# Three chunks of 344 tokens in place of four of 258 in the first half of both output projections

## The chip, the cores and the metric

The kernel runs on one core of a Trainium2 chip. The metric is the device time of one execution in microseconds; before the change it is 2502.07 us, the median of three runs (2500.52, 2502.07 and 2508.82).

## The reference

One inference step of a decoder trunk with two layers, 1024 prompt tokens and 8 decode tokens (one for each of 8 sequences), model width 1024. Each sub-layer adds a gated branch to the residual stream, the gate computed from a conditioning vector:

```
h = h + gate(c) * F(rmsnorm(h) * (1 + scale(c)) + shift(c))
```

In the first layer F is an HGRN2 recurrence with 8 heads of 128, in the second a sliding-window attention (window 128, 16 query heads on 4 key-value heads, sinks, relative bias, a cache for the decode tokens). Each ends in an output projection of 1024 by 1024, which is what the change touches:

```
return o.reshape(bsz, t, D_MODEL).astype(xn.dtype) @ w_o, s_new
```

Each mixer is followed by a SwiGLU feed-forward sub-layer of inner width 2816. Outputs are the trunk's outputs for prompt and decode tokens, the recurrent states and the key-value caches.

## The kernel before

Activations lie with the features on the 128 partitions (8 tiles of 128 features, called k or n) and the tokens along the columns. The 1032 tokens, the decode tokens last, are cut in chunks: `G3` has three of 344 columns, `G4` four of 258. Every product of 128 by 128 weights with a chunk is done as three matmuls (`mm3`, lines 291 to 293), with weights and activations each split in a high and a low part.

The output projection is cut in two halves by its inner dimension: `wo_first` multiplies the first four of the eight mixer outputs, `wo_second` the last four. `wo_first` runs while the mixer's last heads are still being computed: the function `run` takes turns between it and other generators in the proportion of the weights beside them. This happens twice. In stage A (lines 1650 to 1653, about 539 to 634 us) it stands beside the last recurrence head (`hgrn_tail`) and a conditioning product. In stage B (line 1988, about 1613.5 to 1727 us) it stands beside the prompt attention (`second`) and the decode attention (`dec`).

For each chunk and each output tile n, `wo_product` does four `mm3`, that is 12 matmuls, into one PSUM bank. The pool of these banks, `mm`, has four. Then `residual` (line 845, on VectorE) multiplies the bank by the gate and adds it to the residual tile in place; that frees the bank. In the last chunk a further update of 8 columns (line 849) takes the decode tokens.

The residual stands in a `Stack` made on `G4`: eight tiles `hs`, one for each chunk of 258 tokens and each group of four features k. `reload_stack` loads them from DRAM on the queue of SyncE (line 658). In stage A all eight loads come before `run`. In stage B it is a generator in two steps: the two tiles of chunk 0 first, then, after the first steps of `second` and `dec` have issued their own loads on the same queue, the six tiles of chunks 1 to 3. The loads between are the attention's (lines 1854 and 1845), the key and value caches (line 1769) and the new decode rows, which overwrite a row of the cache tiles (line 1774). The decode attention's first matmuls are transposes of the cached keys (line 1781), products with the decode queries (line 1789) and scores of the prompt attention beside them (line 1872). `wo_second` and everything after it stay on `G4` tiles of the residual.

Of the kernel before, what the change touches and what calls it, by code (L numbers as in the profile page):

```python
# [12 lines left out]
ALU = mybir.AluOpType  # L13
# [40 lines left out]
G3, G4 = Grid(344), Grid(258)  # L54
# [11 lines left out]
def trunk_kernel(  # L66
# [40 lines left out]
    pe, act, dve, pool, sp = nc.tensor, nc.scalar, nc.vector, nc.gpsimd, nc.sync  # L107
# [10 lines left out]
    def nm(s):  # L118
        uid[0] += 1
        return f"{s}_{uid[0]}"  # L120

    def big(dt=F32, cols=TOK, parts=P):
        return p4.tile([parts, cols], dt, tag="c4", name=nm("c4"))

    def mmp():
        return pp.tile([P, 512], F32, tag="mm", name=nm("mm"), bufs=4)
# [8 lines left out]
    def axp():  # L135
        return pp.tile([P, 512], F32, tag="ax", name=nm("ax"), bufs=4)

    def small(shape, tag, bufs=2, dt=F32):
        return sm.tile(shape, dt, tag=tag, name=nm(tag), bufs=bufs)
# [8 lines left out]
    class Stream:  # L148
# [15 lines left out]
        def next(self):  # L164
            n, room = self.used + 1, self.look
            while n < len(self.specs) and self.size[n] <= room:
                room -= self.size[n]
                n += 1
            self.ahead(n)
            u = self.done[self.used]  # L170
            self.used += 1
            return u
# [238 lines left out]
    for kk in range(4):  # L411
        t = big(cols=1024)
        wa[0].append(first_half(2 * kk, 0, t))
        t = big(cols=1024)
# [12 lines left out]
    ps = axp()  # L427
# [4 lines left out]
    ps = axp()  # L432
# [16 lines left out]
    res = []  # L449
    hd = cst.tile([P, KT, NB], F32, name="hd")  # L450
    xs = dp.tile([KT, P, T], F32, name="xs")
    ps = axp()
# [4 lines left out]
    ada = cst.tile([P, 112, 9], F32, name="ada")  # L457
# [6 lines left out]
    def ada_step(q, k):  # L464
        u = ca.next()
        if k == 0:
            ada_ps[q] = axp()
        for i in range(2):
            for j in range(4):
                pe.matmul(  # L470
                    ada_ps[q][32 * j : 32 * j + 32, 256 * i : 256 * i + 256],
                    cT[:, k, :],
                    u[i][:, j, :],
                    start=(k == 0 and i == 0),
                    stop=(k == KT - 1 and i == 1),
                    tile_position=(0, 32 * j),
                )

    def ada_end(q):
        a = big(cols=512)  # L480
        act.copy(a, ada_ps.pop(q))
        yield
        ps = axp()
        for b in range(4):
            pe.transpose(ps[:, b * P : (b + 1) * P], a[:, b * P : (b + 1) * P], ident)
        psv = ps.rearrange("p (b j r) -> p b j r", b=4, j=4)
        for b in range(4):
            dve.tensor_tensor(
                adav[:, q, :, b, :],
                psv[:, b, :, 0:9],  # L490
                bc(bTv[:, q, :, b], 2, 9),
                op=ALU.add,
            )
# [33 lines left out]
    def mod_scale(m, ks=slice(0, KT)):  # L527
        _, sc, nw = MODS[m]
        return dve.scalar_tensor_tensor(
            modA[:, m, ks, :],  # L530
            ada[:, sc : sc + KT, :][:, ks, :],
            1.0,
            bc(nT[:, nw : nw + KT][:, ks], 2, 9),
            op0=ALU.add,
            op1=ALU.mult,
        )
# [94 lines left out]
    class Stack:  # L631
# [16 lines left out]
        def at(self, k, g, c):  # L648
            return self.t[c][k // self.m][:, k % self.m, : g.pl[c]]

        def move(self, dram, cs, load):
            for c in cs:
                n, s = self.g.pl[c], self.g.prompt(c)
                for i in self.groups():
                    d = dram[self.rows(i)][:, :, s].rearrange("k p n -> p k n")
                    if load:
                        self.t[c][i] = p4.tile([P, self.m, self.g.w], F32, tag="c4", name=nm("hs"))
                        sp.dma_start(self.part(c, i, n), d)
                    else:
                        sp.dma_start(d, self.part(c, i, n))  # L660
# [180 lines left out]
                yield 1  # L841

    def residual(ps, c, n, gate, tdec, g=G3):
        hc = res[-1].at(n, g, c)
        dve.scalar_tensor_tensor(  # L845
            hc, ps[:, : g.pl[c]], ada[:, gate + n, 0:1], hc, op0=ALU.mult, op1=ALU.add
        )
        if c == g.last:
            dve.tensor_tensor(tdec[:, n, :], ps[:, g.pl[c] : g.w], ada[:, gate + n, 1:9], op=ALU.mult)

    def residual_dec(tdec):
        dve.tensor_tensor(hd, hd, tdec, op=ALU.add)
# [431 lines left out]
    def run(*gens):  # L1284


        left = [[0, g, n] for g, n in gens]
        while left:
            x = min(left, key=lambda e: e[0] / e[2])
            r = next(x[1], "end")  # L1290
            if r == "end":
                left.remove(x)
                continue
            x[0] += r or 1
# [44 lines left out]
    def conditioning(quads, mods):  # L1339

        for q in quads:
            for k in range(KT):
                ada_step(q, k)
                if k % 2:
                    yield
            yield from ada_end(q)
            yield
        for m in mods:
            mod_scale(m)


    def mixed(scr, i):

        o = Rows(4)
        for c in range(NCH):
            n = G3.pl[c]
            for k in range(4):
                xh, xl = (z[:, :n] for z in o.at(k, G3, c))
                t = small([P, W], "w", 6)[:, :n]
                sp.dma_start(t, scr[4 * i + k][:, G3.prompt(c)])  # L1360
                act.copy(xh, t)
                eng = dve if k % 2 or not i else pool
                eng.tensor_tensor(xl, t, xh, op=ALU.subtract)
        return o
# [4 lines left out]
    def wo_product(u, o, c, n, gate, tdec, g=G3, bank=mmp):  # L1369
        ps = bank()  # L1370
        for k in range(4):
            i = 2 * k + n % 2
            xh, xl = o.at(k, g, c)
            mm3(ps[:, : g.w], wcol(u, 0, i), wcol(u, 1, i), xh, xl, k == 0, k == 3)
        residual(ps, c, n, gate, tdec, g)

    def wo_first(o, gate, before_last=None, g=G4):
        tdec = small([P, KT, NB], "tdec", 2)
        us = [ws.next() for _ in range(4)]
        for c in range(g.n):  # L1380
            if c == g.last and before_last:
                before_last()
            for n in range(KT):
                wo_product(us[n // 2], o, c, n, gate, tdec, g)
                if n % 2:
                    yield
        residual_dec(tdec)

    def wo_second(o, gate, m, back, beside=iter(()), end=(3, 5)):
        tdec = small([P, KT, NB], "tdec", 2)  # L1390
        us = [ws.next() for _ in range(4)]
        st = res[-1]
        N = StackNorm(st)
        x = Quads()

        def then(c):
            st.move(back, [c], False)
            yield from N.finish(c, *((3, 8) if c < G4.last else end))
            yield LAG
            yield from N.apply_steps(c, m, x)  # L1400

        for c in range(G4.n):
            for n in range(KT):
                wo_product(us[n // 2], o, c, n, gate, tdec, G4, anyp)
                N.square(c, n)
                step()
                if c and ((c - 1) * KT + n) % 2 == 0:
                    next(beside, None)
            if c == G4.last:
                residual_dec(tdec)  # L1410
                N.square_dec()
            queue(then(c))
        for _ in beside:
            pass
        return x, st
# [65 lines left out]
    def ffn(l, x, st, hs, norm, aside=None):  # L1481
# [126 lines left out]
        for c in range(NCH):  # L1608
            for n in range(KT):
                ps = mmp()  # L1610
                for k in range(2):
                    xh, xl = o.at(k, G3, c)
                    mm3(ps[:, :W], wcol(us[k], 0, n), wcol(us[k], 1, n), xh, xl, k == 0, k == 1)
                residual(ps, c, n, gff, tdec)
# [33 lines left out]
    hgrn_tail = hgrn_core(NH - 1)  # L1648
    o = mixed(osc, 0)
    mixed_dec(o, odec, 0)  # L1650
    for _ in reload_stack(xs, G4):
        pass
    run((wo_first(o, 16), 16), (hgrn_tail, 48), (conditioning((4, 5), (4,)), 12))
    o = mixed(osc, 1)
    mixed_dec(o, odec, 1)
    back = [dp.tile([KT, P, T], F32, name=f"hs{i}") for i in range(2)]
    X, st = wo_second(o, 16, 1, back[0], conditioning((6, 3), (2, 3)))
# [3 lines left out]
    class ToKV(StackNorm):  # L1661
# [9 lines left out]
        def before_last(self):  # L1671
            pass
# [23 lines left out]
    for c in range(NCH):  # L1696
        need(nkv.x, c)
        for n in range(4):
            ps = mmp()
# [9 lines left out]
    for a in range(2):  # L1709
        t = big(cols=T)  # L1710
        for half in range(2):
            ps = axp()
# [5 lines left out]
    ps = axp()  # L1718
# [7 lines left out]
    ps = axp()  # L1726
# [246 lines left out]
    o = mixed(asc, 0)  # L1973
    second = attention(1)
# [3 lines left out]
    dec = decode_attention()  # L1978
# [6 lines left out]
            pass  # L1985
        mixed_dec(o, adec, 0)

    run((wo_first(o, 64, dec_first), 16), (second, 24), (dec, 20))
    o = mixed(asc, 1)
    mixed_dec(o, adec, 1)  # L1990
    X, st = wo_second(o, 64, 4, back[1], end=(5, 5))
# [163 lines left out]
```

## Time and profile before

| | |
|---|---|
| median of three runs | 2502.07 us |
| profiled execution, its own time | 2503.72 us |
| profiled execution, span | 2501.9 us |
| mean granted TensorE clock | 0.995 |
| TensorE busy | 2461.2 us, 98% |
| VectorE busy | 1391.0 us, 56% |
| ScalarE busy | 902.2 us, 36% |

Times in the profile count from the span's start. PE is TensorE, PEld its weight loads, DVE VectorE, ACT ScalarE, POOL GpSimd, SP SyncE; a "q" behind an engine's name is its queue of DMA issues. A matmul's record is longer than the distance to the next start, because matmuls are pipelined. L845 is line 845 of the kernel. A bracket in a timeline row gives the idle time before the row and what ended it.

### The profile page before, as it was taken

To read this page: it belongs to the slowest core of one execution; us is meant where nothing else is said; L and a number is where in the kernel's file an instruction comes from. 1 tells how busy PE (TensorE), PEld (TensorE's weight loads), DVE (VectorE), ACT (ScalarE), POOL (GpSimd) and SP (SyncE) were. 2 spreads that over 40 slices of the span, in tenths; PEclk is the share of its full clock that TensorE was granted. 3 is DMA by queue.
4 is the path that set the end of the run, shared out by engine and by line. 5 is a ranking of instruction groups with operands and counts; after the bars stand their busy time and mean duration, and the time that the engine had idled before them with its cause. 6 is when DMAs were issued, how large, how long until landed. Compare 5 with 4: busy or idle time off the path is not lost.

```text
span 2501.9 us, 52373 instructions
## 1 busy us (share of the span) xinstructions
PE 2461.2 (98%) x21557; PEld 2341.0 (94%) x21557; DVE 1391.0 (56%) x3177; ACT 902.2 (36%) x2012; POOL 774.8 (31%) x560
## 2 busy tenths in 40 slices
PE   7999999999999999999999999999999999999998
PEld 5999999987889999999999998878999999999998
DVE  6444444454586555655433735576885555565436
ACT  5333333331363332333211565454643333333112
POOL 1211111110225444444432121102264444445221
PEclk9999999999999999999999999999999999999999
DMA  9564222258932224226321322523222222264201
GB/s 332 154 206 146 76 79 70 70 167 271 287 114 86 85 85 147 87 83 233 130 68 59 93 56 60 158 88 110 77 85 77 77 77 77 82 232 145 68 26 69
DMA packets 314561, 293.43 MB, mean 117 GB/s; under 512 B 28681, under 2 KB 291738, under 8 KB 314290
## 3 DMA queue, kind: packets, MB, share of 16 engines
q1 hardware_dynamic: 313920, 289.86, 36.0%
q8 instruction: 170, 2.79, 0.5%
q14 instruction: 69, 0.57, 0.1%
q10 hardware_dynamic: 402, 0.22, 0.0%
HBM read 231.27 MB, written 63.99 MB: 118 GB/s over the span
## 4 chain that ended last, share of the span: by engine, by line
PE 90%; DVE 4%; issue 2%; DMA 2%; ACT 1%; POOL 0%; ACTq 0%; SPq 0%; DVEq 0%; POOLq 0%
PE mm L291 20%; PE mm L293 20%; PE mm L292 20%; PE ax L291 6%; PE ax L293 6%; PE ax L292 6%; PE ax L470 2%; PE ax L1943 1%; PE ax L1098 1%; PE ax L1872 1%; PE ax L1929 1%; DMA raw<-in_w_ffn_in_dram 1%; PE ax L1188 1%; PE ax L1225 1%; PE ax L1224 1%
## 5 line engine op out<-in xcount | busy, mean ns | idle before, releaser
L185 POOL TENSOR_TENSOR wu<-raw,wu 128x512 fp32r<-128x512 f32 x460 | 628.3, 1373 | 1451.6 <-ACT wu L182 1355.1
L291 PE MATMUL mm<-c,wu 128*128 128x344 f32 (+1 forms) x2104 | 674.7, 321 | 2.4 <-ACT c L917 1.7
L292 PE MATMUL mm<-c,wu 128*128 128x344 f32 (+1 forms) x2104 | 662.8, 315 | 0.3 <-DVE c L920 0.3
L293 PE MATMUL mm<-c,wu 128*128 128x344 f32 (+1 forms) x2104 | 661.4, 314 | 0.0
L182 ACT CAST wu<-raw 128x512 fp32r<-128x512 f32 x464 | 286.0, 620 | 678.9 <-PE mm L293 369.8
L291 PEld LDWEIGHTS mm<-c,wu 128*128 128x128 f32 x2104 | 398.0, 189 | 14.8 <-issue 8.6
L292 PEld LDWEIGHTS mm<-c,wu 128*128 128x128 f32 x2104 | 398.6, 189 | 5.1 <-issue 3.4
L293 PEld LDWEIGHTS mm<-c,wu 128*128 128x128 f32 x2104 | 398.5, 189 | 2.5 <-issue 2.4
L291 PE MATMUL mm<-xq,wu 128*128 128x258 f32 x1376 | 390.6, 284 | 2.3 <-ACT wu L182 1.0
L293 PE MATMUL mm<-xq,wu 128*128 128x258 f32 x1376 | 389.4, 283 | 0.8 <-POOL wu L185 0.8
L292 PE MATMUL mm<-xq,wu 128*128 128x258 f32 x1376 | 388.8, 283 | 1.2 <-DVE xq L838 1.2
L291 PE MATMUL ax<-xq,wu 128*128 128x258 f32 x1120 | 317.5, 283 | 0.0
L293 PE MATMUL ax<-xq,wu 128*128 128x258 f32 x1120 | 316.7, 283 | 0.0
L292 PE MATMUL ax<-xq,wu 128*128 128x258 f32 x1120 | 316.5, 283 | 0.0
L291 PEld LDWEIGHTS mm<-xq,wu 128*128 128x128 f32 x1376 | 260.1, 189 | 3.9 <-ACT wu L182 1.2
L292 PEld LDWEIGHTS mm<-xq,wu 128*128 128x128 f32 x1376 | 261.2, 190 | 1.7 <-DVE xq L838 1.6
L293 PEld LDWEIGHTS mm<-xq,wu 128*128 128x128 f32 x1376 | 260.2, 189 | 2.4 <-issue 1.2
L845 DVE SCALAR_TENSOR_TENSOR hs<-mm,ada,hs 128x344 f32<-128x344 f32 (+3 forms) x228 | 120.6, 532 | 182.4 <-PE mm L293 173.5
L292 PEld LDWEIGHTS ax<-xq,wu 128*128 128x128 f32 x1120 | 212.5, 190 | 0.0
L293 PEld LDWEIGHTS ax<-xq,wu 128*128 128x128 f32 x1120 | 212.0, 189 | 0.0
L291 PEld LDWEIGHTS ax<-xq,wu 128*128 128x128 f32 x1120 | 211.7, 189 | 0.0
L845 DVE SCALAR_TENSOR_TENSOR c<-mm,ada,c 128x344 f32<-128x344 f32 (+1 forms) x132 | 74.7, 570 | 111.7 <-PE mm L293 110.7
(329 smaller groups left out, 3607.6 us busy)
## 6 DMA issues: line engine op xcount, KB each, us to landing
c<-in_w_ada_dram SPq DMA_DIRECT2D x96, 512.0 KB
raw<-in_w_ffn_in_dram SPq DMA_DIRECT2D x160, 256.0 KB
ff<-c SPq DMA_DIRECT2D x44, 516.0 KB
c<-ff SPq DMA_DIRECT2D x44, 516.0 KB
raw<-in_w_ffn_out_dram SPq DMA_DIRECT2D x44, 512.0 KB
raw<-in_w_in_a_dram SPq DMA_DIRECT2D x32, 512.0 KB
hs<-hs SPq DMA_DIRECT2D x16, 516.0 KB
out_dram<-c SPq DMA_DIRECT2D x16, 512.0 KB
```

The lines of the kernel that those rows point to most:

```text
L182: i = act.copy(u[:, 0, :], src)
L185: j = eng.tensor_tensor(u[:, 1, :], src, u[:, 0, :], op=ALU.subtract)
L291: put(pe.matmul(ps, wh, xh, start=first, stop=False))
L292: put(pe.matmul(ps, wh, xl, start=False, stop=False))
L293: put(pe.matmul(ps, wl, xh, start=False, stop=last))
L470: pe.matmul(ada_ps[q][32 * j : 32 * j + 32, 256 * i : 256 * i + 256], cT[:, k, :], u[i][:, j, :], start=(k == 0 and i == 0), stop=(k == KT ...
L845: dve.scalar_tensor_tensor(hc, ps[:, : g.pl[c]], ada[:, gate + n, 0:1], hc, op0=ALU.mult, op1=ALU.add)
L1098: pe.matmul(ps[32 * j : 32 * j + 32, c * 32 : (c + 1) * 32], KS[:, t0 : t0 + 32], QP[:, t0 : t0 + 32], start=True, stop=True, tile_positio ...
L1188: pe.matmul(ps[:, j * P : (j + 1) * P], kt[:, s], vt[:, s], start=True, stop=True)
L1224: pe.matmul(o, QP[:, s], S[:, (c - 1) * P : c * P], start=True, stop=False)
L1225: pe.matmul(o, attT[:, c, :], vt[:, s], start=(c == 0), stop=True)
L1872: pe.matmul(psv[hf][:, gi, s0:256], q[2 * gp + gi][r, tb * P : (tb + 1) * P], kT[a][r, (tb - 1) * P + s0 : (tb + 1) * P], start=True, stop ...
```

## The change

`wo_first` takes `G3` as its default grid, so it works in three chunks of 344 tokens: 24 products of 12 matmuls in each stage in place of 32. The residual tiles keep the cut of `G4`. Where the grid of the product and that of the stack differ, `residual` asks the stack for `pieces`: chunk 0 (tokens 0 to 343) gives 258 columns in tile 0 and 86 in tile 1, chunk 1 gives 172 in tile 1 and 172 in tile 2, chunk 2 gives 86 in tile 2 and 250 in tile 3. One instruction is issued for each piece. The weight of `wo_first` in both calls of `run` goes from 16 to 12, its number of steps.

```diff
+        def pieces(self, k, g, c):
+
+            s = g.prompt(c)
+            for i in range(self.g.n):
+                p = self.g.prompt(i)
+                a, b = max(s.start, p.start), min(s.stop, p.stop)
+                if a < b:
+                    t = self.t[i][k // self.m]
+                    yield a - s.start, t[:, k % self.m, a - p.start : b - p.start]
+
...
     def residual(ps, c, n, gate, tdec, g=G3):
-        hc = res[-1].at(n, g, c)
-        dve.scalar_tensor_tensor(
-            hc, ps[:, : g.pl[c]], ada[:, gate + n, 0:1], hc, op0=ALU.mult, op1=ALU.add
-        )
+        st = res[-1]
+        same = not isinstance(st, Stack) or st.g is g
+        for j, hc in [(0, st.at(n, g, c))] if same else st.pieces(n, g, c):
+            dve.scalar_tensor_tensor(
+                hc, ps[:, j : j + hc.shape[-1]], ada[:, gate + n, 0:1], hc, op0=ALU.mult, op1=ALU.add
+            )
...
-    def wo_first(o, gate, before_last=None, g=G4):
+    def wo_first(o, gate, before_last=None, g=G3):
...
-    run((wo_first(o, 16), 16), (hgrn_tail, 48), (conditioning((4, 5), (4,)), 12))
+    run((wo_first(o, 16), 12), (hgrn_tail, 48), (conditioning((4, 5), (4,)), 12))
...
-    run((wo_first(o, 64, dec_first), 16), (second, 24), (dec, 20))
+    run((wo_first(o, 64, dec_first), 12), (second, 24), (dec, 20))
```

Lines after the insertions stand 10 to 12 further down in the changed kernel: line 845 becomes 857, 1781 becomes 1793, 1789 becomes 1801, 1872 becomes 1884.

On VectorE at the start of stage B, before the change, hs_18556 is the tile of chunk 0 with features 0 to 3, hs_18558 that with features 4 to 7, and hs_18593 the tile of chunk 1 with features 0 to 3; mm is the PSUM bank of a product:

```order
L845 SCALAR_TENSOR_TENSOR hs_18556<-mm_18642,ada,hs_18556 128x258
L845 SCALAR_TENSOR_TENSOR hs_18556<-mm_18656,ada,hs_18556 128x258
L845 SCALAR_TENSOR_TENSOR hs_18556<-mm_18730,ada,hs_18556 128x258
L845 SCALAR_TENSOR_TENSOR hs_18556<-mm_18744,ada,hs_18556 128x258
L845 SCALAR_TENSOR_TENSOR hs_18558<-mm_18802,ada,hs_18558 128x258
L845 SCALAR_TENSOR_TENSOR hs_18558<-mm_18816,ada,hs_18558 128x258
L845 SCALAR_TENSOR_TENSOR hs_18558<-mm_18922,ada,hs_18558 128x258
L845 SCALAR_TENSOR_TENSOR hs_18558<-mm_18936,ada,hs_18558 128x258
L845 SCALAR_TENSOR_TENSOR hs_18593<-mm_19006,ada,hs_18593 128x258
```

The same place after the change, where hs_18468 and hs_18470 are the two tiles of chunk 0 and hs_18505 and hs_18507 the two of chunk 1:

```order
L857 SCALAR_TENSOR_TENSOR hs_18468<-mm_18554,ada,hs_18468 128x258
L857 SCALAR_TENSOR_TENSOR hs_18468<-mm_18569,ada,hs_18468 128x258
L857 SCALAR_TENSOR_TENSOR hs_18468<-mm_18644,ada,hs_18468 128x258
L857 SCALAR_TENSOR_TENSOR hs_18468<-mm_18659,ada,hs_18468 128x258
L857 SCALAR_TENSOR_TENSOR hs_18505<-mm_18554,ada,hs_18505 128x86
L857 SCALAR_TENSOR_TENSOR hs_18505<-mm_18569,ada,hs_18505 128x86
L857 SCALAR_TENSOR_TENSOR hs_18505<-mm_18644,ada,hs_18505 128x86
L857 SCALAR_TENSOR_TENSOR hs_18505<-mm_18659,ada,hs_18505 128x86
L857 SCALAR_TENSOR_TENSOR hs_18470<-mm_18767,ada,hs_18470 128x258
```

Before, the first update on a tile of chunk 1 is the ninth of the stage; now it is the fifth, and it reads the bank of the first product.

On TensorE, before the change, the first decode matmuls (L1781) stand after 141 matmuls of the projection, inside its twelfth product (mm_19153):

```order
L293 MATMUL mm_19153<-c_2194_18502,wu_18088 128x258
L291 MATMUL mm_19153<-c_2196_18504,wu_18091 128x258
L292 MATMUL mm_19153<-c_2197_18505,wu_18091 128x258
L293 MATMUL mm_19153<-c_2196_18504,wu_18091 128x258
L1781 MATMUL ax_18582<-ident,c_2218_18568 128x128 x4
L291 MATMUL mm_19153<-c_2198_18506,wu_18091 128x258
L292 MATMUL mm_19153<-c_2199_18507,wu_18091 128x258
L293 MATMUL mm_19153<-c_2198_18506,wu_18091 128x258
L1789 MATMUL ax_18581<-late,c_2225_18587 128x8 x4
```

After the change they stand after 48, between the fourth product (mm_18659) and the fifth (mm_18767):

```order
L291 MATMUL mm_18659<-c_2190_18418,wu_18003 128x344
L292 MATMUL mm_18659<-c_2191_18419,wu_18003 128x344
L293 MATMUL mm_18659<-c_2190_18418,wu_18003 128x344
L1793 MATMUL ax_18494<-ident,c_2210_18480 128x128 x4
L1801 MATMUL ax_18493<-late,c_2217_18499 128x8 x4
L1884 MATMUL ax_18586<-c_1902_16449,c_2206_18472 128x128
L1884 MATMUL ax_18587<-c_1902_16449,c_2206_18472 128x128
L1884 MATMUL ax_18586<-c_1902_16449,c_2207_18474 128x128
L1884 MATMUL ax_18587<-c_1902_16449,c_2207_18474 128x128
L1793 MATMUL ax_18596<-ident,c_2210_18480 128x128 x4
L291 MATMUL mm_18767<-c_2184_18412,wu_18319 128x344
```

The last row is the fifth product's first matmul; its bank is one that the update of the first product has to give back.

## Rows read from the trace of the kernel before

**Rows 1.** The page: busy time, share of the span and number of instructions of each engine, and the shares of the chain that ended last by engine.

```profile
PE 2461.2 (98%) x21557; PEld 2341.0 (94%) x21557; DVE 1391.0 (56%) x3177; ACT 902.2 (36%) x2012; POOL 774.8 (31%) x560
...
PE 90%; DVE 4%; issue 2%; DMA 2%; ACT 1%; POOL 0%; ACTq 0%; SPq 0%; DVEq 0%; POOLq 0%
```

**Rows 2.** TensorE's matmuls grouped by line and shape, over the whole span: output and inputs, count, busy us and mean ns of one, idle time before them and what ended it. The lines 292 and 293 have as many each. Of the 384 with 258 columns on line 291, 128 belong to `wo_first` in each of the two stages and the rest to `wo_second`.

```profile
L291 PE MATMUL mm<-c,wu 128*128 128x344 f32 x1720 | 561.0, 326 | 1.7 <-ACT c L917 1.7
...
L291 PE MATMUL mm<-c,wu 128*128 128x258 f32 x384 | 113.8, 296 | 0.7 <-DVE hs L845 0.7
```

**Rows 3.** SyncE's queue of DMA issues from 1602 us: start, duration, the line that issues, what it loads, count of issues in the row.

```profile
1607.78 0.94 SPq L658 DMA_DIRECT2D hs<-hsc  x1
...
1612.43 0.37 SPq L658 DMA_DIRECT2D hs<-hsc  x1
...
1616.24 2.69 SPq L1769 DMA_DIRECT2D c<-in_cache_swa_k_dram  x2
1618.98 3.49 SPq L1769 DMA_DIRECT2D c<-in_cache_swa_v_dram  x2
1625.21 4.74 SPq L1774 DMA_DIRECT2D c<-nd  x4
1630.00 4.13 SPq L658 DMA_DIRECT2D hs<-hsc  x6
```

**Rows 4.** VectorE's timeline in the same stretch: start, duration, line, operation, output and inputs, count, idle time before.

```profile
1617.81 1.26 DVE L845 SCALAR_TENSOR_TENSOR hs<-mm,ada,hs 128x258 f32<-128x258 f32 x3
...
1625.29 0.49 DVE L845 SCALAR_TENSOR_TENSOR hs<-mm,ada,hs 128x258 f32<-128x258 f32 x1 [0.95 <-PE mm L293]
1634.20 1.67 DVE L845 SCALAR_TENSOR_TENSOR hs<-mm,ada,hs 128x258 f32<-128x258 f32 x4 [8.43 <-DMA hs<-hsc]
```

**Rows 5.** TensorE's timeline: the stage's first matmul, the decode matmuls and what follows them, and the first matmul of `wo_second` (`ax<-c,wu`). From 1613.55 to 1630.50 the three lines of `mm3` have 47 matmuls each.

```profile
1613.55 0.28 PE L291 MATMUL mm<-c,wu 128*128 128x258 f32 x1
...
1630.51 0.60 PE L1781 MATMUL ax<-ident,c 128*128 128x128 f32 x4
...
1631.78 1.06 PE L1789 MATMUL ax<-late,c 128*128 128x8 f32 x8 [0.32 <-ACT c L1785]
...
1633.41 0.66 PE L1781 MATMUL ax<-ident,c 128*128 128x128 f32 x4
1634.74 0.42 PE L291 MATMUL mm<-c,wu 128*128 128x258 f32 x1 [0.67 <-DVE hs L845]
1634.96 0.42 PE L292 MATMUL mm<-c,wu 128*128 128x258 f32 x1
...
1638.19 0.37 PE L292 MATMUL mm<-c,wu 128*128 128x258 f32 x1
1638.39 0.29 PE L293 MATMUL mm<-c,wu 128*128 128x258 f32 x1
...
1727.02 0.29 PE L291 MATMUL ax<-c,wu 128*128 128x258 f32 x1
```

**Rows 6.** TensorE's waits over the whole span: who waits for whom, us in total, number of times, the longest.

```profile
PE ax L1098 <- issue: 4.4, 2, 3.1
...
PE mm L291 <- DVE hs L845: 0.7, 1, 0.7
```

**Rows 7.** Two windows in which TensorE runs matmuls of one shape, 258 columns in the first and 344 in the second: length, busy us and number of records of PE, PEld, DVE, ACT and POOL, granted clock, DMA share, GB/s.

```profile
850.00:900.00 50.00, 50.00 (x419) 50.00 (x418) 28.58 (x56) 16.68 (x34) 22.39 (x18) 1.00 0.29 92
1250.00:1300.00 50.00, 50.00 (x319) 50.00 (x318) 19.16 (x40) 10.25 (x14) 16.66 (x11) 1.00 0.22 75
```

**Rows 8.** The chain of waits from 1612 to 1645 us: start, duration, what the end waited for.

```profile
1620.69 8.63 DMA c<-in_cache_swa_v_dram
...
1630.00 4.11 DMA hs<-hsc
```

**Rows 9.** The updates of the residual on VectorE grouped by shape, and those of the decode tokens (L849); columns as in rows 2.

```profile
L845 DVE SCALAR_TENSOR_TENSOR hs<-mm,ada,hs 128x344 f32<-128x344 f32 x88 | 50.2, 574 | 79.4 <-PE mm L293 79.2
...
L845 DVE SCALAR_TENSOR_TENSOR hs<-mm,ada,hs 128x258 f32<-128x258 f32 x72 | 34.3, 483 | 57.8 <-PE mm L293 49.0 <-DMA hs<-hsc 8.4
...
L849 DVE TENSOR_TENSOR tdec<-mm,ada 128x8 f32<-128x8 f32 x112 | 17.2, 154 | 0.0
...
L845 DVE SCALAR_TENSOR_TENSOR hs<-mm,ada,hs 128x250 f32<-128x250 f32 x24 | 11.3, 469 | 7.7 <-PE mm L293 7.7
```

**Rows 10.** One window from the end of the slow restart to the end of stage B; columns as in rows 7.

```profile
1638.40:1727.00 88.60, 88.31 (x682) 66.16 (x682) 71.18 (x298) 56.03 (x196) 11.31 (x10) 1.00 0.22 67
```

**Rows 11.** Stage A: SyncE's queue, and VectorE's first update of the residual in the stage.

```profile
536.29 3.32 SPq L658 DMA_DIRECT2D hs<-xs  x5
...
545.94 2.09 SPq L658 DMA_DIRECT2D hs<-xs  x3
...
545.54 0.48 DVE L845 SCALAR_TENSOR_TENSOR hs<-mm,ada,hs 128x258 f32<-128x258 f32 x1
```

**Rows 12.** Windows of stage A; columns as in rows 7, the last three being granted clock, DMA share and GB/s.

```profile
544.00:545.00 1.00, 1.00 (x7) 1.00 (x6) 0.80 (x2) 0.00 (x0) 0.00 (x0) 0.50 1.10 349
545.00:546.00 1.00, 1.00 (x7) 1.00 (x6) 1.00 (x3) 0.00 (x0) 0.00 (x0) 0.50 0.73 229
...
550.00:600.00 50.00, 45.54 (x766) 37.65 (x753) 24.30 (x55) 8.46 (x27) 0.00 (x0) 0.97 0.81 264
```

## The prediction

> **What bounds the kernel now.** First the busy totals and the line of shares by engine in the chain that ended last: TensorE is busy in 98% of the span and carries 90% of the chain [rows 1]. So time is won only by fewer TensorE cycles, and lost wherever TensorE stands. Next the groups of matmuls by shape: both stages that change (I call them A, beside the last recurrence head, and B, beside the attention) run the 258-column products, 384 matmuls each; the form of 344 columns is there too, in other stages [rows 2]; 384 is 4 chunks by 8 output tiles by 12 matmuls. Then the stretch itself on three engines. In B the SyncE queue issues the residual's tiles of chunk 0 before 1613, then the loads of the decode attention, and only at 1630.00 the tiles of chunks 1 to 3 [rows 3]. VectorE does the eight residual updates of chunk 0 by 1625.8 and then waits 8.43 us for the tile of chunk 1 [rows 4]. TensorE does not notice: it runs 141 projection matmuls from 1613.55, the first decode matmuls at 1630.51, the last three of the twelfth product, and waits only 0.67 us at 1634.74 for a free bank [rows 5, 6]. The before kernel just covers a late load.
>
> **The matmuls themselves.** In two stretches of matmuls of one shape TensorE starts 419 of 258 columns in 50 us and 319 of 344 columns in 50 us: 0.1193 and 0.1567 us each [rows 7]. A stage is 384 x 0.1193 = 45.8 us before and 288 x 0.1567 = 45.1 us after: 0.7 us less in a stage where nothing else changes, all on the path, since TensorE is the bound.
> The 0.7 is a difference of two long rows, 0.463 against 0.456 ns per column [rows 7]. The Trainium skill ("TensorE: Matmul & The Clock Gate", section "Wait — 56ns, not 53.3ns?") puts a warm matmul at its columns over 2.4 GHz plus about 2.5 ns whatever its size; my estimate from that is 110.0 and 145.8 ns, so 96 fewer matmuls are worth 0.25 us in a stage. By the page the change would give back even less than by the rows; the rows decide.
>
> **The new wait in B.** A chunk of 344 tokens needs the 258 columns of residual tile 0 and 86 columns of tile 1. The residual on VectorE is what frees a bank, and there are four banks. In the changed order the first four products are followed on VectorE by four pieces of 258 columns and then by the four pieces of 86 columns in tile 1; the fifth product's first matmul takes a bank that the first of these pieces gives back. SyncE's order does not change: tile 1 is issued at 1630.00, behind the cache and new-row loads, whose own chain holds the queue: the load of the cached values ends 8.63 us after 1620.69, then the new rows are issued, then the tiles, which land 4.11 us after 1630.00 [rows 3, 8]. Nothing in that chain depends on the projection, so the landing stays near 1634.1.
> TensorE therefore stops after 4 x 12 x 0.1567 = 7.5 us, at 1613.55 + 7.5 = 1621.1. Queued behind the waiting product on TensorE are all later matmuls; ahead of it stand the first decode matmuls (transposes of the cached keys, scores), about 3 us of work that waits for the new rows issued from 1625.21 on and so falls inside the gap, with room to end before 1634. When tile 1 lands VectorE needs one piece of 86 columns. That form is not in the trace. Bounds: 0.15 us (the decode update of 8 columns from the same bank [rows 9]) and 0.48 us (258 columns); from 574 ns at 344 and 483 ns at 258 [rows 9] the slope is 1.06 ns per column, so 86 columns come to 483 - 182 = 0.30 us, which I take. TensorE restarts at 1634.74 - (0.48 - 0.30) = about 1634.55.
> What is then left: before, 32 - 12 = 20 products of 258 columns, 240 matmuls; after, 24 - 4 = 20 products of 344 columns, 240 matmuls. The difference is 240 x (0.1567 - 0.1193) = 9.0 us. This holds both what the longer stop loses and what the fewer columns gain in this stage. With the earlier restart B ends 9.0 - 0.2 = 8.8 us later, after the 1727.02 at which the second half starts now [rows 5].
> The clock after the wait costs nothing more: already before, matmuls of 258 columns stand 0.215 us apart from 1634.74 to 1638.19, the lower of the two clock levels, and 0.12 us apart from 1638.39 [rows 5]. The wait is longer now but the restart comes at the same time and I let it climb as fast. If it takes as long again, 3.5 us at half pace, that costs 1.7 us more; if it were not low at all, 1.7 us less.
>
> **VectorE's pieces.** Each product has two residual instructions instead of one: 48 in a stage instead of 32. Before 24 x 0.483 + 8 x 0.469 = 15.3 us; after, with 0.30 for 86, 0.39 for 172 and 0.47 for 250 columns, 8 x (0.48 + 0.30 + 0.39 + 0.39 + 0.30 + 0.47) = 18.6 us, 3.3 us more busy time. From the end of the restart to the end of B TensorE is busy 88.31 of 88.60 us and VectorE 71.18 [rows 10]; with 3.3 more it stays below TensorE. I take 0. If that cover is gone in the softmax's dense parts the price is those 3.3 us.
>
> **Stage A.** The same crossing, but there the five loads of the first tiles are issued from 536.29 on, before the stage, and the first update of the residual is only at 545.54 [rows 11]; at 545 to 546 the transfer rate already falls, from 349 to 229 GB/s, while the last tiles of these five land [rows 12]. So tile 1 is there when its first piece comes, and the stage gains its 0.7 us. The other three loads are issued at 545.94; the second chunk's products need them only after eight products more, and the 24 share the stage with other work. TensorE's waits in A are another matter: 4.4 us in two waits at L1098 for no event that the profile shows, the longer 3.1 us [rows 6]. The new interleaving sets other work around them; from the rows they can go (4.4 less) or come again as much (4.4 more). I take 0.
>
> **Sum.** +8.8 in B, -0.7 in A, 0 for VectorE: +8.1 us. The profiled execution took 2503.72 (span 2501.9), so 2511.8 by it; it stood 1.65 above the median 2502.07, so against the median I forecast 2510.2, 0.32% slower. 0.3% (7.5 us) is about what a measurement of this kernel can tell from no change, so "slower" begins at 2509.6.
>
> **Rivals.**
> 1. Not slower: the 9.0 us are given back. Mechanism: beside the attention TensorE's matmuls interleave with softmax steps whose pace VectorE sets (71.18 of 88.60 busy [rows 10]); more projection left over would fill gaps there instead of lengthening the stretch. For it: TensorE's busy time is modelled and can hide gaps. Against it: that stretch shows 0.29 us idle and the waits of TensorE name none of it [rows 6, 10]. It decides if at least 8.1 us of gaps exist there. Time 2510.2 - 9.0 = 2501.2. Chance 0.10.
> 2. A's waits without a visible cause vanish with the other interleaving. 4.4 us, and the 1.5 us that the lowered clock costs in that stretch (0.97 over 50 us [rows 12] is 3 us at half pace): 2510.2 - 5.9 = 2504.3. For it: nothing in the program asks for them. Against: the small matmuls of 32 columns that show them stay. Chance 0.13.
> 3. Worse than forecast: the wait comes, and VectorE's extra pieces (3.3) hold the banks in the dense part or the clock stays low as long again (1.7): all of both is 2510.2 + 5.0 = 2515.2, half of both 2512.7; I put it at 2514. Chance 0.12.
> 4. The banks don't matter and a matmul is worth its busy record: a mean of 296 ns at 258 columns against 326 at 344 [rows 2], 2 x (384 x 0.296 - 288 x 0.326) = 39.6 us faster, 2463. Against it: the records overlap, starts stand 0.12 us apart while a record lasts 0.28 [rows 5], so the distance of starts counts. Chance 0.03.
> Forecast as it stands: 0.62, its own range 2507 to 2514.
>
> **How the numbers follow.** Faster: rival 4 and a remainder, 0.04. Same (2494.6 to 2509.6): rivals 1 and 2, 0.23, and about a third of the forecast, whose centre stands only 0.6 us above the bound, 0.22: 0.45. Slower: the other two thirds of it and rival 3, 0.51. The range leaves out rivals 1 and 4 and little else: 2503 to 2515.
>
> **What would show it.** Right: in the changed profile TensorE's waits name the residual's line with one wait of several us that ends near 1634 (0.7 earlier), its release a piece of 86 columns, which itself waited for the load of tile 1; the second half of the projection starts some 8 us later than 1727. The starts of 344-column matmuls 0.157 us apart. In A no wait of the residual for a load. Wrong: tile 1 lands well before 1634, or TensorE shows the wait and B still ends at its old time (rival 1), or waits at L1098 are gone (rival 2).

## The result, and the profile after

The changed kernel takes 2512.14 us (median of ten runs, 2509.35 to 2521.28), the kernel before 2501.96 (ten runs beside it, 2500.12 to 2508.82). The ratio is 1.0042, with a 95% interval of 1.0032 to 1.0052: 0.42% slower, some 10 us. The forecast was 2510.2, 0.32% slower.

The profiled execution of the changed kernel has a span of 2512.9 us. First its TensorE waits over the whole span (who waits for whom, us in total, times, longest), to be held against [rows 6]:

```profile
PE ax L1793 <- DMA c<-nd: 8.2, 1, 8.2
PE ax L428 <- DVE c L424: 5.8, 1, 5.8
PE ax L1110 <- issue: 3.2, 2, 2.2
...
PE mm L292 <- issue: 0.9, 1, 0.9
```

One wait of 8.2 us is new and stands first. It is not that of a projection matmul on the residual: it is the first decode matmul (line 1793), which waits for the new decode rows. Then TensorE's timeline around it, answering to [rows 5]:

```profile
1613.97 0.32 PE L291 MATMUL mm<-c,wu 128*128 128x344 f32 x1
...
1621.22 0.32 PE L292 MATMUL mm<-c,wu 128*128 128x344 f32 x1
1621.38 0.31 PE L293 MATMUL mm<-c,wu 128*128 128x344 f32 x1
1629.86 1.09 PE L1793 MATMUL ax<-ident,c 128*128 128x128 f32 x4 [8.17 <-DMA c<-nd]
1631.62 1.88 PE L1801 MATMUL ax<-late,c 128*128 128x8 f32 x8 [0.68 <-ACT c L1797]
1633.43 1.23 PE L1884 MATMUL ax<-c,c 64*128 64x128 f32 x8
1634.58 1.11 PE L1793 MATMUL ax<-ident,c 128*128 128x128 f32 x4
1635.35 0.63 PE L291 MATMUL mm<-c,wu 128*128 128x344 f32 x1
1635.78 0.49 PE L292 MATMUL mm<-c,wu 128*128 128x344 f32 x1
...
1639.43 0.32 PE L293 MATMUL mm<-c,wu 128*128 128x344 f32 x1
...
1736.84 0.28 PE L291 MATMUL ax<-c,wu 128*128 128x258 f32 x1
```

The first row is the first matmul of stage B. TensorE stops after 1621.38, has its decode matmuls from 1629.86 to 1635.35, and takes up the fifth product only then. The last row is the first matmul of the second half, which stood at 1727.02. VectorE in the same stretch, answering to [rows 4]:

```profile
1619.85 0.49 DVE L857 SCALAR_TENSOR_TENSOR hs<-mm,ada,hs 128x258 f32<-128x258 f32 x1 [1.41 <-PE mm L293]
1621.73 0.48 DVE L857 SCALAR_TENSOR_TENSOR hs<-mm,ada,hs 128x258 f32<-128x258 f32 x1 [1.39 <-PE mm L293]
1634.35 0.95 DVE L857 SCALAR_TENSOR_TENSOR hs<-mm,ada,hs 128x86 f32<-128x86 f32 x4 [12.13 <-DMA hs<-hsc]
```

After the fourth piece of 258 columns VectorE stands 12.13 us until the tile of chunk 1 has landed, where it stood 8.43 before. SyncE's queue, answering to [rows 3], is the old one: the caches, the new rows, then the tiles.

```profile
1619.15 3.43 SPq L1781 DMA_DIRECT2D c<-in_cache_swa_v_dram  x2
1625.41 4.74 SPq L1786 DMA_DIRECT2D c<-nd  x4
1630.21 4.19 SPq L668 DMA_DIRECT2D hs<-hsc  x6
```

Windows of the two kernels price it (length; busy us and records of PE, PEld, DVE, ACT, POOL; granted clock; DMA share; GB/s). In the kernel before: the 141 matmuls, the decode matmuls, the slow restart, and stage B whole.

```profile
1613.55:1630.51 16.96, 16.96 (x144) 16.96 (x143) 5.76 (x14) 2.54 (x6) 1.67 (x2) 1.00 0.91 294
1630.51:1634.74 4.23, 3.25 (x29) 2.66 (x27) 0.54 (x2) 1.17 (x2) 0.00 (x0) 1.00 0.88 235
1634.74:1638.39 3.65, 3.65 (x17) 3.65 (x18) 1.95 (x7) 0.04 (x1) 0.00 (x0) 0.53 1.10 354
...
1613.55:1727.02 113.47, 112.20 (x869) 89.46 (x867) 79.44 (x319) 59.81 (x204) 12.98 (x12) 0.98 0.38 117
```

In the changed kernel: the 48 matmuls, the stop, the decode matmuls, the slow restart, and stage B whole.

```profile
1613.97:1621.60 7.63, 7.63 (x50) 7.44 (x48) 3.42 (x10) 2.47 (x7) 2.60 (x2) 1.00 1.00 340
1621.60:1629.86 8.26, 0.09 (x2) 0.04 (x1) 0.48 (x1) 0.00 (x0) 0.00 (x0) 0.75 0.91 295
1629.86:1635.35 5.49, 4.82 (x25) 4.17 (x25) 0.95 (x4) 0.59 (x1) 0.00 (x0) 0.50 0.76 209
1635.35:1639.43 4.08, 4.08 (x16) 4.08 (x15) 0.25 (x1) 0.59 (x1) 0.00 (x0) 0.51 1.09 358
...
1613.97:1736.84 122.87, 113.89 (x773) 89.83 (x771) 79.63 (x335) 59.02 (x205) 14.11 (x12) 0.94 0.37 113
```

Stage B is 122.87 - 113.47 = 9.4 us longer. Of these 7.7 are TensorE idle (122.87 - 113.89 = 8.98 against 1.27) and 1.7 are busy time, most of it in the decode matmuls: they now run at a granted clock of 0.50, the 1.2 GHz level, for 4.82 us of busy time against 3.25 at 1.00 (in a window that also holds three projection matmuls). A slow restart follows in both. The projection's columns are the same.

The chain that ended last, from 1620 to 1640 us, says what the restart hung on (start, duration, what the end waited for):

```profile
1625.41 4.30 DMA c<-nd
...
1629.86 1.10 PE ax L1793 x4
```

TensorE had two reasons to stand. No bank came free before the end of the first piece of 86 columns, at 1634.65; and the decode matmuls that stand ahead of the fifth product waited for the new rows until 1629.86 and then ran until 1635.35. The second ended last, by 0.7 us.

### The profile page after: what moved, and what is told of

Read it like the earlier page. It is cut to its first block, busy times and chain, and to the rows that moved or that the text cites. A ratio compares the mean times of both kernels' runs of the same rounds, so it can differ in the third digit from the quotient of the medians.

```text
span 2512.9 us, 52008 instructions
## 1 busy us (share of the span) xinstructions
PE 2462.5 (98%) x21365; PEld 2340.3 (93%) x21365; DVE 1395.2 (56%) x3209; ACT 901.2 (36%) x2012; POOL 773.5 (31%) x560
## 4 chain that ended last, share of the span: by engine, by line
PE 89%; DVE 3%; DMA 3%; issue 2%; ACT 1%; POOL 0%; SPq 0%; ACTq 0%; DVEq 0%; POOLq 0%
PE mm L291 20%; PE mm L293 19%; PE mm L292 19%; PE ax L291 6%; PE ax L293 6%; PE ax L292 6%; PE ax L470 2%; PE ax L1955 1%; PE ax L1884 1%; PE ax L1110 1%; PE ax L1941 1%; DMA raw<-in_w_ffn_in_dram 1%; PE ax L1237 1%; PE ax L1200 1%; DMA gd<-rd 1%
## 5 line engine op out<-in xcount | busy, mean ns | idle before, releaser
L291 PE MATMUL mm<-c,wu 128*128 128x344 f32 (+1 forms) x2040 | 662.7, 325 | 1.7 <-ACT c L929 1.7
L292 PE MATMUL mm<-c,wu 128*128 128x344 f32 (+1 forms) x2040 | 651.0, 319 | 1.4 <-issue 0.9
L293 PE MATMUL mm<-c,wu 128*128 128x344 f32 (+1 forms) x2040 | 650.3, 319 | 0.0
L291 PEld LDWEIGHTS mm<-c,wu 128*128 128x128 f32 x2040 | 384.9, 189 | 12.9 <-issue 8.1
L292 PE MATMUL mm<-xq,wu 128*128 128x258 f32 x1376 | 389.3, 283 | 1.3 <-DVE xq L848 1.3
L293 PEld LDWEIGHTS mm<-c,wu 128*128 128x128 f32 x2040 | 385.2, 189 | 5.0 <-issue 5.0
L292 PEld LDWEIGHTS mm<-c,wu 128*128 128x128 f32 x2040 | 385.4, 189 | 4.6 <-issue 2.8
L292 PE MATMUL ax<-xq,wu 128*128 128x258 f32 x1120 | 316.0, 282 | 0.0
L292 PEld LDWEIGHTS mm<-xq,wu 128*128 128x128 f32 x1376 | 261.2, 190 | 1.7 <-DVE xq L848 1.7
L857 DVE SCALAR_TENSOR_TENSOR hs<-mm,ada,hs 128x344 f32<-128x344 f32 (+5 forms) x260 | 124.2, 493 | 187.2 <-PE mm L293 174.1
L292 PEld LDWEIGHTS ax<-xq,wu 128*128 128x128 f32 x1120 | 212.5, 190 | 0.0
```

Source lines behind the costliest of these rows:

```text
L291: put(pe.matmul(ps, wh, xh, start=first, stop=False))
L292: put(pe.matmul(ps, wh, xl, start=False, stop=False))
L293: put(pe.matmul(ps, wl, xh, start=False, stop=last))
L857: dve.scalar_tensor_tensor(hc, ps[:, j : j + hc.shape[-1]], ada[:, gate + n, 0:1], hc, op0=ALU.mult, op1=ALU.add)
```

## The experiments

For each kernel the two stages are read from its own profile. A stage begins with the projection's first matmul and ends with the first matmul of the second half; the start of A is taken 2.81 us after the first load of the residual tiles, as it is in the kernel before. The times are medians, the ratios those to the kernel before run on the same chip.

| kernel | A, us | B, us | TensorE idle in B | time, us | ratio (95%) |
|---|---|---|---|---|---|
| before | 94.59 | 113.47 | 1.27 | 2501.96 | |
| changed | 91.50 | 122.87 | 8.98 | 2512.14 | 1.0042 (1.0032 to 1.0052) |
| changed, tile 1 early | 91.14 | 111.57 | 1.35 | 2501.28 | 0.9999 (0.9989 to 1.0008) |
| before, tile 1 early | 92.46 | 110.50 | 0.02 | 2502.24 | 0.9996 (0.9987 to 1.0006) |
| change in A alone | 91.21 | 113.79 | 1.61 | 2503.90 | 1.0007 (0.9999 to 1.0016) |
| change in B alone | 96.19 | 122.89 | 9.66 | 2515.80 | 1.0050 (1.0037 to 1.0063) |
| before, tile 1 early, updates in two pieces | 92.21 | 110.42 | 0.02 | 2501.45 | 0.9994 (0.9986 to 1.0002) |
| before, chunk 0 late too | 93.51 | 121.00 | 8.42 | 2513.95 | 1.0042 (1.0026 to 1.0057) |
| A changed, B as before, tile 1 early | 92.04 | 110.49 | 0.03 | 2501.56 | 0.9995 (0.9985 to 1.0006) |
| changed, three banks for chunk 0 | 91.60 | 122.69 | 10.60 | 2515.1, one run | |

**Tile 1 early, in the changed kernel.**

```diff
-    def reload_stack(src, g):
+    def reload_stack(src, g, first=1):
...
-        st.move(src, [0], True)
+        st.move(src, range(first), True)
         yield
-        st.move(src, range(1, g.n), True)
+        st.move(src, range(first, g.n), True)
...
-    loads = reload_stack(hsc, G4)
+    loads = reload_stack(hsc, G4, 2)
```

> The changed kernel, but in stage B the residual tiles of chunks 0 and 1 are both loaded in the first step, ahead of the attention's and the decode attention's loads. Theory (the late tile 1 fills the four banks and stops TensorE): the stop at 1621 goes, the decode matmuls move behind it, and B falls from 122.9 to about 113 us; time about 2512 - 9.5 = 2502.5, and chunk 1's second pieces may wait up to 2 us for tile 2. Rival (the longer B comes from the extra VectorE pieces or from the new interleaving with the attention): B stays at 121 us or more, time 2510 or more.

Measured: 2501.28, B 111.57. The rival is out as a cause of its own: with the same products, pieces and weights of `run`, the loss is gone when two DMAs stand earlier in a queue. VectorE's timeline shows how it went:

```profile
1617.98 1.13 DVE L857 SCALAR_TENSOR_TENSOR hs<-mm,ada,hs 128x86 f32<-128x86 f32 x4 [1.44 <-DMA hs<-hsc]
1619.84 0.70 DVE L857 SCALAR_TENSOR_TENSOR hs<-mm,ada,hs 128x258 f32<-128x258 f32 x2 [0.73 <-PE mm L293]
```

SyncE's queue of the same kernel has the tiles of chunk 1 in its first row, together with the second tile of chunk 0:

```profile
1610.97 1.48 SPq L668 DMA_DIRECT2D hs<-hsc  x3
1612.54 1.89 SPq L1866 DMA_DIRECT2D c<-qsc  x2
...
1626.71 5.17 SPq L1786 DMA_DIRECT2D c<-nd  x4
1631.93 2.34 SPq L668 DMA_DIRECT2D hs<-hsc  x4
```

The first piece of 86 columns still waits for its tile, 1.44 us, but at 1617.98 instead of 1634.35, while TensorE runs on. The new rows are issued 1.3 us later than in the changed kernel, at no visible cost. TensorE's timeline shows why, and what is left of the wait for a bank:

```profile
1632.59 0.60 PE L1793 MATMUL ax<-ident,c 128*128 128x128 f32 x4
...
1638.38 0.43 PE L291 MATMUL mm<-c,wu 128*128 128x344 f32 x1 [0.80 <-DVE hs L857]
```

The edit moves loads only, but the order on TensorE's queue moved with them: the first decode matmuls now stand behind 130 projection matmuls, where it was 48 in the changed kernel, and the new rows are there when their turn comes. So the run shows that the late load is the cause of the loss. It does not tell apart the two ways in which it held TensorE, the bank and the decode matmuls put ahead of the fifth product.

**The same early load in the kernel before.** The diff is the one above.

> The kernel before with the same early load of chunks 0 and 1 in stage B. Theory: the four-chunk kernel just covered the late load, so it gains at most the 0.67 us of bank wait and the 1.7 us of low clock after 1634: 2500 to 2502. Rival (the early load is worth 9 us to any version, because it frees the queue or starts the decode work at another time): 2493.

Measured: 2502.24, 0.24 above the theory's range, which is less than the scatter; B is 110.50, 3.0 less than before, with the bank wait and the low clock gone, but no gain shows in the timed runs (their interval still has room for 3 us). The 10 us that the early load brings to the changed kernel are therefore not a gain that any version would have. The window of stage B in the changed kernel with tile 1 early:

```profile
1612.07:1723.64 111.57, 110.22 (x772) 86.68 (x771) 79.47 (x334) 59.88 (x205) 14.19 (x13) 1.00 0.40 126
```

And the window of stage B in the kernel before with tile 1 early:

```profile
1613.16:1723.66 110.50, 110.48 (x869) 88.06 (x867) 79.49 (x319) 59.23 (x203) 14.39 (x12) 1.00 0.38 117
```

Both run at a granted clock of 1.00 and without the stop, so the busy time compares the two cuts as a whole: 110.22 against 110.48 us, 0.26 less. That is not the price of 96 matmuls alone, because the attention's matmuls stand in another order in the two kernels. Counted from each start to the next, idle time left out, the projection takes 48.2 us in three chunks and 48.9 in four, 0.7 less, and the 482 other matmuls take 62.0 and 61.6, 0.4 more. With its 1.35 us of idle time the stage is still 1.07 us longer in three chunks.

**The change in one stage alone.**

```diff
-    run((wo_first(o, 64, dec_first), 12), (second, 24), (dec, 20))
+    run((wo_first(o, 64, dec_first, G4), 16), (second, 24), (dec, 20))
```

> The change in stage A alone; stage B runs on four chunks of 258 as before. Theory: the forecast gave A 0.7 us less; the changed profile shows 91.5 against 94.6 us, of which 1.7 look like clock after a wait that fell otherwise: so 2499 to 2501.5. Rival (A's 3.1 us are a chance of this one profile, or A also pays for its pieces): 2502 or more.

```diff
-    run((wo_first(o, 16), 12), (hgrn_tail, 48), (conditioning((4, 5), (4,)), 12))
+    run((wo_first(o, 16, None, G4), 16), (hgrn_tail, 48), (conditioning((4, 5), (4,)), 12))
```

> The change in stage B alone; stage A runs on four chunks as before. Theory: the whole loss is in B, so 2502 + 9.4 = 2511.4, at or a little above the changed kernel. Rival (part of the 10 us comes from A or from the stretch between the stages): 2508 or less.

Measured: 2503.90 for A alone, 2515.80 for B alone. The loss is in B, as the theory had it; its time is even above the changed kernel's, with six runs between 2509.87 and 2517.73. For A the theory's 2499 to 2501.5 is missed: the profile has A at 91.21, 3.4 us shorter than before, and the timed runs show no gain (1.0007, 0.9999 to 1.0016; the interval leaves room for a gain of 0.3 us at most).

**Two pieces on four chunks.**

```diff
-        dve.scalar_tensor_tensor(
-            hc, ps[:, : g.pl[c]], ada[:, gate + n, 0:1], hc, op0=ALU.mult, op1=ALU.add
-        )
+        m = g.pl[c]
+        for a, b in [(0, m)] if cut is None else [(0, cut), (cut, m)]:
+            dve.scalar_tensor_tensor(
+                hc[:, a:b], ps[:, a:b], ada[:, gate + n, 0:1], hc[:, a:b], op0=ALU.mult, op1=ALU.add
+            )
...
-        residual(ps, c, n, gate, tdec, g)
+        residual(ps, c, n, gate, tdec, g, 172 if bank is mmp else None)
```

> Four chunks of 258 in both stages and the early load of the run before last (chunks 0 and 1 first), but each residual update of wo_first is cut in two pieces of 172 and the rest: 64 VectorE instructions in a stage instead of 32, 32 more, twice as many as the change adds. Theory (pieces lie beside TensorE): B stays at 110.5 us and the time at 2502.2, within 1 us. Rival (pieces hold the banks and cost up to 0.2 us each): B 114 to 117, time 2506 to 2512 with both stages.

The edit of the early load is in this run too. The cut goes by the bank, so it also doubles 192 updates of the feed-forward's output product. Measured: 2501.45, B 110.42, VectorE's records in B 350 against 319 and its busy time 81.93 us against 79.49:

```profile
1613.20:1723.62 110.42, 110.40 (x869) 88.06 (x867) 81.93 (x350) 59.30 (x203) 13.55 (x12) 1.00 0.39 119
```

256 more VectorE instructions in the kernel cost nothing that can be measured. Where TensorE is not stopped, the pieces show no price.

**Chunk 0 late too, in the kernel before.**

```diff
-    next(loads)
     next(second)
     dec = decode_attention()
     next(dec)
+    next(loads)
```

> The kernel before (four chunks, one tile for each chunk), but in stage B the residual tiles of chunk 0 too are issued behind the attention's and the decode's loads. Theory (a late tile with four banks stops TensorE after four products, whatever the chunk): TensorE stops after 4 x 1.43 = 5.7 us near 1619, restarts near 1635 with 28 products of 258 left in place of 20: 28 x 1.432 = 40.1 us against 37.6 in the changed kernel, so B about 125 us and the time about 2513 to 2515. Rival (the loss belongs to the three-chunk cut, not to the late tile): B stays near 113.5, time 2502.

Measured: 2513.95, B 121.00. A four-chunk kernel with one whole tile for each chunk now shows the same picture in TensorE's timeline:

```profile
1620.87 0.28 PE L293 MATMUL mm<-c,wu 128*128 128x258 f32 x1
1628.14 1.09 PE L1781 MATMUL ax<-ident,c 128*128 128x128 f32 x4 [6.99 <-DMA c<-nd]
...
1633.94 0.58 PE L291 MATMUL mm<-c,wu 128*128 128x258 f32 x1
```

It began at 1615.22, so it stops after 5.8 us, four products of 1.43. B is 4 us shorter than expected, since the queue without the tiles of chunk 0 in front reaches the late tiles earlier:

```profile
1629.09 7.28 SPq L658 DMA_DIRECT2D hs<-hsc  x8
```

That is 13.9 us after the stage's start, against 16.2 in the changed kernel (1630.21 - 1613.97), and the restart comes 18.7 us after the start (1633.94 - 1615.22), against 21.4 (1635.35 - 1613.97). The time is as expected all the same, and that is luck: the profiled execution's span is 11.8 us above the kernel before's (2513.7 against 2501.9), of which B has 7.5; where the other 4.3 come from is not shown. What the three-chunk cut does is make the first chunk need a late tile; the late tile with four banks is what costs. Here too the first decode matmuls stand right behind the four products and wait for the new rows.

**A changed, B on four chunks with tile 1 early.** The edit of the first experiment together with the one that leaves the change in stage A alone.

> Stage A in three chunks as changed, stage B in four chunks of 258 with chunks 0 and 1 loaded early. Theory: A takes 91.2 us and B 110.5, as in the two profiles with these halves, 3.4 and 3.0 less than before; the stretch between the stages takes back about 1.3: 2497. Rival (A's gain in the profiles does not reach the end, as A alone was timed at 2503.9): 2501 to 2504.

Measured: 2501.56. The two stages are as short as expected (92.04 and 110.49), and the time is the rival's. It is no better than the kernel before (0.9995, 0.9985 to 1.0006).

**Three banks.**

```diff
+        if hold:
+            kept = mmp()
+            pe.transpose(kept[:, 0:P], ident, ident)
...
+            if hold and c == 0:
+                dve.tensor_tensor(tdec[:, 0, :], kept[:, 0:NB], res[-1].t[1][0][:, 3, 0:NB], op=ALU.add)
...
-    run((wo_first(o, 64, dec_first), 12), (second, 24), (dec, 20))
+    run((wo_first(o, 64, dec_first, hold=True), 12), (second, 24), (dec, 20))
```

> The changed kernel with one of the four banks held, in stage B only, by a small transpose until the first four products have been added to the residual. Theory (the number of banks sets how far TensorE gets before the late tile): the stop comes after three products, 36 matmuls, 5.6 us after the start of the stage, and 21 products of 344 columns are left instead of 20: B 122.9 + 1.9 = 124.8 us. Rival (TensorE is held by the new decode rows in its queue, not by banks): the wait ends at the same time and the number of products before it doesn't matter to the end of B beyond noise, B 122.9.

Measured: TensorE does 36 matmuls and stops, at 1614.81 + 5.9:

```profile
1614.81 0.40 PE L291 MATMUL mm<-c,wu 128*128 128x344 f32 x1
...
1629.95 1.09 PE L1798 MATMUL ax<-ident,c 128*128 128x128 f32 x4 [9.21 <-DMA c<-nd]
...
1635.44 0.64 PE L291 MATMUL mm<-c,wu 128*128 128x344 f32 x1
```

So the banks do set how far it gets. The price was not the expected one: B is 122.69 us, the rival's 122.9 and not 124.8. Here B started 0.75 us nearer to the new rows' landing (15.14 us before its first decode matmul, 15.89 in the changed kernel), and the 21 products after the restart took 102.06 us (1635.44 to 1737.50) where 20 took 101.49. One more product of 1.88 us lengthened the rest by 0.57. The count of matmuls fits the theory and the end of B the rival. What TensorE waits for is again the new rows, for a decode matmul that now stands behind 36 projection matmuls instead of 48. So the run shows that the banks set where TensorE stops, but not that a free bank alone would have let it go on.

## Why the prediction was right

**The place and the mechanism.** Right, and shown by three runs: the early load takes the loss away, the early load alone gives nothing to the kernel before, and a late tile does the same to the four-chunk kernel. In all of them the place of the decode matmuls on TensorE's queue moved with the load, so they show the late tile as the cause, and not how much of the stop the bank would have made without the decode matmuls ahead. That the bank alone would have held TensorE until 1634.65 is read from VectorE's row and from the order of the program; no run tries it. The stop came after four products at 1621.6 (forecast 1621.1, with the stage starting 0.4 later), the tile at 1634.35 (forecast 1634.1), and the piece of 86 columns takes 302 ns (forecast 0.30):

```profile
L857 DVE SCALAR_TENSOR_TENSOR hs<-mm,ada,hs 128x86 f32<-128x86 f32 x32 | 9.4, 302 | 26.9 <-PE mm L293 14.6 <-DMA hs<-hsc 12.1
```

**The size in B.** 9.4 us against 8.8. The step that was off is the one on the decode matmuls, "about 3 us of work that waits for the new rows issued from 1625.21 on and so falls inside the gap, with room to end before 1634". They started only at 1629.86, since the first load of new rows took 4.30 us from 1625.41, and ran at the lower clock, 5.49 us to 1635.35. So TensorE restarted 0.8 us later than forecast, held by its own queue and not by the tile, whose first piece was done by 1634.65. With it falls "The clock after the wait costs nothing more": the restart's own slow stretch is little longer than before (4.08 us against 3.65), but the decode matmuls pay 4.82 us of busy time for 3.25. From the restart to the end of B the forecast has 101.3 us (1634.55 to 1735.8), and 101.49 were measured.

**The sum.** The total came out near because B did, and otherwise with some luck. The two profiled executions differ by 11.0 us: 2.6 before A, -3.1 in A, 0.9 between the stages, 9.4 in B, 1.2 behind it. The forecast had -0.7 in A and nothing outside the stages. Without B the measured parts come to 1.6 us because they nearly cancel, and the profiles of the other kernels scatter as much there: A begins between 539.1 and 542.8 us, and what follows B takes 774.5 to 777.5.

**What would show it.** The sign named beforehand, a wait named after the residual's line, did not appear. The waits view names the instruction that stands first in the queue, here the decode matmul; that VectorE's residual was waiting is read from VectorE's row of 12.13 us. Without that row the wait would be put down to the new rows alone, and the early tile shows that they are not the cause by themselves: they are issued 1.3 us later there, the decode matmuls stand further back, and TensorE does not stand.

**The matmuls.** 0.7 us in a stage was right for the matmuls themselves. In B the starts stand 120.3 ns apart at 258 columns ((1630.51 - 1613.55) / 141) and 157.7 at 344 ((1621.38 - 1613.97) / 47), so a stage is 46.2 us before and 45.4 after, 0.8 less; over the whole stage, in the two kernels with tile 1 early, the projection takes 0.7 us less. What the forecast left out is the attention beside it, whose matmuls stand in another order and take 0.4 us more, so that TensorE's busy time in B falls by 0.26 only. The Trainium skill ("TensorE: Matmul & The Clock Gate", section "Wait — 56ns, not 53.3ns?") puts a fixed cost of about 2.5 ns on each matmul, from which the prediction's estimate was 0.25 us. The trace does not agree: the starts stand 120.3 and 157.7 ns apart where that estimate has 110.0 and 145.8, and the measurement decides.

**VectorE's pieces.** 0 was right, as far as four chunks can show it: 256 more of them cost nothing that the timed runs tell (0.9994, 0.9986 to 1.0002).

**Stage A.** The forecast had 0.7 us less. The five profiles with three chunks in A have 91.1 to 92.0 us, the five with four chunks 92.2 to 96.2: a bigger gain than forecast, and a steadier time. Its waits at L1110 for no visible event did not vanish (3.2 us in two waits, with 0.9 more at L292), so rival 2 is out. A part of A's gain is taken back at once: from the end of A to the start of B the kernels with three chunks take 980.8 to 981.8 us, those with four 978.7 to 981.5 (means 981.2 and 980.2), and TensorE there waits 0.6 to 1.6 us for a load of the conditioning weights, against 0 to 0.5. The rest, some 1 to 2 us, does not show in the timed runs of A alone or of the last combination, whose intervals are about 2 us to either side; whether it is real or the profiles' scatter stays open.

**Rival 1**, that the lost matmuls are given back beside the attention, did not hold: B kept its 9.4 us. The run with three banks shows that there is something in it all the same, 1.3 of 1.88 us (below), though not by gaps that were filled: TensorE idles 0.71 us there after the restart, against 0.14 in the changed kernel.

## What to carry to other kernels

When a loop's chunks are made larger than the tiles that its last step writes to, look at when the second tile is loaded, not only at the first: the first chunk then needs a load that the smaller chunk needed much later. A kernel without waits in a stretch can stand at the edge of one; how many instructions run between the start and the landing, against how many the banks allow, tells how near it is. And the remedy is read off the DMA queue: two loads moved ahead of twelve others won the whole loss back, and gave the kernel that had no loss nothing that the timed runs could tell. Such a move can shift the order on the compute engines' queues as well, so read that order again after it.

## What was not expected of the hardware

After the stop in the three-bank run, 252 projection matmuls and the same attention matmuls took hardly longer than 240 did: TensorE's busy time in the rest of the stage is 101.35 us in both, although the 12 more are worth 1.88. The busy time of the attention's groups fell, while the mean of one stayed. The attention's three groups on TensorE in the changed kernel, from the restart at 1635.35 to the end of B:

```profile
L1955 PE MATMUL ax<-c,c 128*64 128x256 f32 x120 | 19.5, 394 | 0.1
L1884 PE MATMUL ax<-c,c 64*128 64x256 f32 x112 | 18.8, 404 | 0.0
L1941 PE MATMUL ax<-ident,c 128*128 128x128 f32 x120 | 18.0, 282 | 0.0
```

The same groups with three banks, from 1635.44 on (lines 1955, 1884 and 1941 are 1960, 1889 and 1946 there):

```profile
L1960 PE MATMUL ax<-c,c 128*64 128x256 f32 x120 | 18.8, 393 | 0.6 <-DVE amx L1900 0.5
L1946 PE MATMUL ax<-ident,c 128*128 128x128 f32 x120 | 17.7, 281 | 0.1
L1889 PE MATMUL ax<-c,c 64*128 64x256 f32 x112 | 17.7, 404 | 0.0
```

Together 54.2 against 56.3 us for the same 352 matmuls; from each start to the next they take 48.6 us against 51.0. A group's busy time counts overlapping records once, so the same mean with a lower sum says that records of a group overlap one another more. It is no scatter: with the change in B alone the same three groups, from 1637.75 to the end of B, have 19.5, 18.8 and 18.0 us as in the changed kernel. The price of these matmuls goes by the order in which they stand; which part of the order does it, was not tried.

The other is the clock: TensorE stood from 1621.6, and when the decode matmuls came at 1629.86 the granted clock was already 0.50 and stayed there until 1639.4. In the kernel before the same matmuls ran at 1.00, directly behind the projection.
